# The opening of a hybrid diffusion layer: conditioning pages and context norm written as a pipeline by quarters

## The chip, the cores and the metric

The kernel runs on one core of a Trainium2 chip. The metric is device microseconds of one execution, the median of several runs. A profiled execution, taken apart from those runs, gives the trace from which all durations below come.

The engines are called by the profile's names: PE is TensorE (matmuls; PEld is its weight loads), DVE is VectorE, ACT is ScalarE, POOL is GpSimd, and SP is the engine whose queue issues the DMAs.

## The reference

One layer works on 1024 latent tokens and 256 context tokens with 1024 channels each. A conditioning vector passes through SiLU and one large matrix (`w_ada`, 1024 x 9216, fp32) and gives nine vectors of 1024 values (shift, scale and gate for three sublayers), once for the latent stream and once for the context. The first sublayer is a half SwiGLU feed-forward block, and for the context it reads, cut to what matters:

```python
mods   = split(silu(c)           @ w_ada + b_ada, 9)
mods_c = split(silu(c_ctx)[None] @ w_ada + b_ada, 9)
hn = ctx * rsqrt(mean(ctx * ctx, -1) + 1e-6) * g_ffn1
hn = hn * (1 + mods_c[1]) + mods_c[0]
a, b = split(hn @ w_ffn1_in, 2)          # 1024 -> 2 x 2816
hc = ctx + 0.5 * mods_c[2] * ((silu(a) * b) @ w_ffn1_out)
```

The latent stream goes through the same sublayer, then both through the token mixing (an mLSTM and a spatial-gating branch), and the latent stream through a second feed-forward block and a final norm. All is fp32 at the interface.

## The kernel before

**Number format.** Large products are made in a fast 32-bit matmul format (`fp32r` in the profile) whose operands are split into a high part (ACT casts it) and a low part (DVE subtracts it from the source). The helper `split` (lines 147 to 150) does that. A full product is then three matmuls: high by high, high by low, low by high.

**Where the program starts.** Activations are held with channels on the 128 partitions, so 1024 channels are eight tiles. The program first computes the context's half of the first feed-forward input projection (22 pairs of output tiles `pa` and `pb`, 24 matmuls of 128x256 each: eight channel tiles by three products), and beside it prepares the latent stream. Before any such matmul can run it needs the context's normalized and modulated tiles `hnc`, and these need two things: the reciprocal root of the context's mean square, and the shift and scale vectors out of `w_ada`. This is the opening stage (lines 823 to 956).

**The conditioning pages.** Only the first 2048 of the 9216 columns are needed here. They come in four quarters, each of 256 shift and 256 scale columns. A quarter is eight channel tiles `k` of 128x512. `ada_pages` (L826) fetches them two to a page, each page by two DMAs of 256 KB (in rows of 1 KB). `ada_mm` (L837) splits every `k` into high and low (L841 on ACT, L843 on DVE) and multiplies it with the conditioning vectors as the stationary operand of 4 or 2 columns (L844, L845), accumulating into one PSUM tile `adr`. `ada_out` (L848) copies `adr` to SBUF (L850, ACT), turns its rows into columns with eight small fp32 matmuls (L853, tile `adc`), adds the bias (L857) and forms the scales (L864), for the latent stream (q = 0) and the context (q = 1). `mods0` then calls `mod0` for the quarter's two channel tiles: `Norm.mod` (L231 on) multiplies by scale and norm (L233, DVE), adds the shift on ACT and makes the high and low parts of `hnc`. On even tiles this takes two ACT steps and a POOL subtraction (L235 to L237), on odd ones an ACT and a DVE step (L239, L240).

**The context's norm.** `Norm.sq` squares the eight tiles on ACT (L199, L203) and adds them on DVE (L204). `rstd` sums over partitions with PE (L209), takes the reciprocal root of 128x2 values by Newton steps on DVE (L742 to L751) and spreads the result back over the partitions with a diagonal matrix and PE (L218, L222).

**Weights.** Class `Weights` streams the 44 pages of the projection (512 KB each): `fetch` issues the DMA (L122), `load` splits a page into `hl` (L149, L150), with a ring of four `hl`. The first four pages are fetched between the second and the third quarter. The opening runs `proj_k` (L918 to L922) for the first three output tiles in pieces, as `hnc` tiles become ready. The loop over `f` (L974) then goes on with tile after tile (L176), and queues the latent stream's position add (L901), squares, norm and factor pages behind them.

**What sets the order.** Each engine executes its instructions in the order of its queue. That order is chosen by a scheduler when the program is built: it may move instructions against the order of the code where no data dependence forbids it. Buffers come from pools in rotation: twelve 128x512 tiles `t2` for short-lived values, four PSUM banks `mm`, four `sm`, and eight pages each under `pg0` and `pg1`, which hold conditioning pages first and raw weights afterwards.

**Table warm-ups.** At two places (L700, used twice, and L2033) an activation of one column is written ahead of a norm, to have ACT load the square-root table.

Of the kernel before, what the change touches and what calls it, by code (L numbers as in the profile page):

```python
# [9 lines left out]
F32 = mybir.dt.float32  # L10
# [30 lines left out]

COST = lambda f: getattr(f, 'cost', 512)
# [14 lines left out]
def _build(ctx, tc, nc, a, out):  # L57
# [47 lines left out]

    class Weights:


        def __init__(self, order, name, depth, ahead):
            self.c = ExitStack()  # L110
            self.pool = self.c.enter_context(tc.tile_pool(name=name, bufs=1, reuse_waits="tile"))
            self.order = deque(order)
            self.depth, self.ahead = depth, ahead
            self.raws = deque()
            self.ready = deque()

# [30 lines left out]
    def split(hl, src):  # L147
        dv(hl.shape[-1])
        S.copy(hl[:, 0, :], src)  # L149
        V.tensor_sub(hl[:, 1, :], src, hl[:, 0, :].bitcast(F32))  # L150
# [427 lines left out]
    class Stage:  # L578
# [76 lines left out]
        def outp(self, name, graw, gring, gate, nlo, lo_rows, final, keep, tick=None, halves=1, first=None):  # L655
# [23 lines left out]
            def post(p, pts):  # L679
# [19 lines left out]
                elif p == 6:  # L699
                    S.activation(warm, epst, AF.Sqrt)  # L700
# [57 lines left out]
    c4 = cp.tile([128, 8, 4], F32R, name="c4")  # L758
    ck = sc2.rearrange("p q k -> p k q")
    S.copy(c4[:, :, 0:2], ck)  # L760
    V.tensor_sub(c4[:, :, 2:4], ck, c4[:, :, 0:2].bitcast(F32))
    pick = t2("pick", shape=(4, 2))
# [63 lines left out]
    def ada_pages(qt):  # L826
        pages = []
        for kp in range(NKT // KP):
            pg = hnp.tile([128, KP, 2, QW], F32, name="adapg", tag=f"pg{1 - qt // 2}", bufs=8)
            for i in range(KP):  # L830
                src = a["w_ada"][kp * KP + i].rearrange("p (m c) -> p m c", m=9)[:, 0:2, qt * QW:(qt + 1) * QW]
                nc.sync.dma_start(pg[:, i], src)
            pages.append(pg)
        return pages

    def ada_mm(pages):
        pr = sm_ps("adr")  # L837
        for k in range(NKT):
            src = pages[k // KP][:, k % KP].rearrange("p m c -> p (m c)")
            hi = t2("adhi", F32R)  # L840
            S.copy(hi, src)  # L841
            lo = t2("adlo", F32R)
            V.tensor_sub(lo, src, hi.bitcast(F32))  # L843
            T.matmul(pr[0:4, :], c4[:, k, :], hi, start=k == 0, stop=False, skip_group_check=True)  # L844
            T.matmul(pr[0:2, :], c4[:, k, 0:2], lo, start=False, stop=k == NKT - 1, skip_group_check=True)  # L845
        return pr

    def ada_out(qt, pr):  # L848
        row = t2("adrow", shape=(4, 2 * QW))
        S.copy(row, pr[0:4, :])  # L850
        pc = sm_ps("adc")
        for i in range(2 * QD):
            T.matmul(pc[:, 2 * i:2 * i + 2], row[:, i * 128:(i + 1) * 128], pick, start=True, stop=True)  # L853
        sl = slice(qt * QD, (qt + 1) * QD)
        bv = vs_("b_ada").rearrange("p (m d) -> p m d", m=9)
        for q in range(2):
            V.tensor_add(mods[:, 0:2, q, sl],  # L857
                         pc[:, 0:4 * QD].rearrange("p (m d q) -> p m d q", m=2, q=2)[:, :, :, q], bv[:, 0:2, sl])
            scale_mod(0, 1, q, "g_ffn1", sl)
# [11 lines left out]
    def it(f, *args):  # L871
        return lambda: f(*args)
# [20 lines left out]
    def add_pos(tb, d):  # L893
# [7 lines left out]
        V.tensor_tensor(hv, hv, pv, ALU.add)  # L901

    load_c(hc)
    apg = [ada_pages(0), ada_pages(1)]
    for _ in range(4):
        W.fetch(wfirst)
    apg.append(ada_pages(2))
    apg.append(ada_pages(3))
# [4 lines left out]
    nct = Norm(hc, 256, V)  # L913

    def mod0(d):
        nct.mod(d, smod[:, 0, 1, :], mods[:, 0, 1, :], hnc[d][:, 0, :], hnc[d][:, 1, :])

# [6 lines left out]
    def mods0(qt):  # L924
        ada_out(qt, prs[qt])
        for d in range(qt * QD, (qt + 1) * QD):
            mod0(d)

    for d in range(NKT):
        nct.sq(d)  # L930
    prs = [ada_mm(apg[0])]
    nct.rstd()
    prs.append(ada_mm(apg[1]))
    nct.bcast()
    mods0(0)
    for _ in range(4):
        W.load()
    mods0(1)
    first = [W.take("w1i", i) for i in range(3)]
    pf = [mm_ps("pa")[:, :256] for _ in range(3)]  # L940
    for i in range(3):
        proj_k(pf[i], first[i], range(4))
    prs.append(ada_mm(apg[2]))
    mods0(2)
    prs.append(ada_mm(apg[3]))
    proj_k(pf[0], first[0], (4, 5))
    mods0(3)
    for i in (1, 2):
        proj_k(pf[i], first[i], (4, 5))
# [3 lines left out]

    for i in range(3):
        proj_k(pf[i], first[i], (6, 7))
        W.done(wraw)
# [16 lines left out]

    for f in range(NF):  # L974
# [36 lines left out]
        gated = it(gate_c, f, pa, pb)  # L1011
    gated()
# [1020 lines left out]
    S.activation(warm, epst, AF.Sqrt)  # L2033
# [59 lines left out]
def layout(x, c, ctx, c_ctx, w_ada, b_ada, g_ffn1, w_ffn1_in, w_ffn1_out, g_mix, w_in, b_gates,  # L2093
# [43 lines left out]
    r["wsT"] = np.ascontiguousarray(A(w_s)[0].transpose(2, 0, 1)).reshape(128, 512)  # L2137
    r["w_ada"] = np.ascontiguousarray(A(w_ada)[0]).reshape(8, 128, 9216)
# [32 lines left out]
```

## Time and profile before

| | before |
|---|---|
| median of 3 runs | 2672.95 us (2672.78 to 2678.84) |
| profiled execution | 2675.7 us |
| its span, first to last instruction | 2673.9 us |
| PE busy over the span | 2636.7 us (99%) |
| DVE busy over the span | 2025.6 us (76%) |
| DMA: moved in all | 456.74 MB, mean 171 GB/s |

The share of busy time is a mean over stages. In the first 60 us it is different: by stretches of 10 us, PE is busy 0.01, 7.55, 7.19, 6.16, 7.90 and 9.91 us, though the records of a matmul overlap the next and a busy PE can be a slowly fed one. The column PEclk of the view by windows is the share of the full clock that was granted to PE.

In rows of the timeline the columns are start and length in microseconds, engine, line, operation, output<-input, shapes and count, and in brackets the idle time before and what ended it. Rows of groups read: line, engine, operation, output<-input, shapes, count, then busy time and mean length in ns, then idle time before them.

### The profile page before, as it was taken

What the parts mean: (1) busy time and instruction counts of PE and PEld (TensorE: products, weight loads), DVE (VectorE), ACT (ScalarE), POOL (GpSimd) and SP (SyncE); (2) the same over time, 40 slices, a digit from 0 to 9 for tenths busy, and PEclk for the clock granted to TensorE, in tenths of its full rate; (3) what the DMA queues carried; (4) which work ended last, traced back from release to release, by engine and by line L of the source; (5) the groups of instructions that cost most, each with busy time, mean ns of one, the idle gap of its engine ahead of it and who ended that gap; (6) DMA issues with size and microseconds to landing.
All of it is one profiled execution on the core that took longest, in us unless ns stands there. A gap on an engine that the chain in (4) does not pass through costs nothing.

```text
span 2673.9 us, 35709 instructions
## 1 busy us (share of the span) xinstructions
PE 2636.7 (99%) x12734; PEld 2205.5 (82%) x12734; DVE 2025.6 (76%) x3643; ACT 1103.7 (41%) x1895; POOL 127.6 (5%) x214
## 2 busy tenths in 40 slices
PE   6999999999999999999999999999999999999998
PEld 4998888888889878888888888888887888888887
DVE  6898888788969647788775888677568877776855
ACT  6673333334337525554443342112245433334432
POOL 0000000000000000000000005442000000000000
PEclk9999999999999999999999999999999999999999
DMA  8943454359578222246553477458241433237545
GB/s 276 354 160 107 147 169 138 130 192 319 192 233 278 92 79 90 103 148 215 190 169 110 143 226 268 155 172 284 81 146 35 154 126 130 107 126 271 190 159 172
DMA packets 199585, 456.74 MB, mean 171 GB/s; under 512 B 20592, under 2 KB 49008, under 8 KB 199408
## 3 DMA queue, kind: packets, MB, share of 16 engines
q1 hardware_dynamic: 199408, 454.47, 50.4%
q8 instruction: 100, 1.64, 0.3%
q14 instruction: 77, 0.63, 0.1%
HBM read 328.95 MB, written 125.51 MB: 170 GB/s over the span
## 4 chain that ended last, share of the span: by engine, by line
PE 88%; DVE 5%; DMA 3%; issue 2%; ACT 1%; SPq 0%; POOL 0%; POOLq 0%; ACTq 0%; DVEq 0%
PE qb L401 20%; PE pq L1322 14%; PE po L527 13%; PE qa L401 10%; PE pt L1796 10%; PE pr L1233 6%; PE pa L176 2%; PE pb L176 2%; PE pc L1104 2%; PE pn L1909 2%; PE pu L1635 2%; DMA adapg<-in_w_ada_dram 1%; PE pkc L1302 1%; PE pn L1907 1%; PE pvc L1393 1%
## 5 line engine op out<-in xcount | busy, mean ns | idle before, releaser
L149 ACT CAST ring<-rawq 128x512 fp32r<-128x512 f32 x432 | 265.9, 620 | 533.9 <-PE qb L401 190.3
L527 PE MATMUL po<-gring,wring 128*128 128x512 f32 (+1 forms) x1896 | 425.7, 385 | 1.0 <-DMA gring<-fsp 0.7
L527 PEld LDWEIGHTS po<-gring,wring 128*128 128x128 f32 x1896 | 349.3, 188 | 73.3 <-issue 1.4
L150 DVE TENSOR_TENSOR ring<-rawq,ring 128x512 fp32r<-128x512 f32 x432 | 295.9, 689 | 131.4 <-ACT ring L149 129.6
L401 PE MATMUL qb<-fc,ring 128*128 128x512 f32 x1440 | 339.9, 389 | 0.4 <-DVE u L422 0.2
L401 PEld LDWEIGHTS qb<-fc,ring 128*128 128x128 f32 x1440 | 269.8, 188 | 58.0 <-DVE u L422 2.2
L401 PE MATMUL qa<-fa,ring 128*128 128x512 f32 x1056 | 252.9, 390 | 0.0
L401 PEld LDWEIGHTS qa<-fa,ring 128*128 128x128 f32 x1056 | 198.1, 188 | 41.5 <-issue 0.5
L401 PE MATMUL qb<-fb,ring 128*128 128x512 f32 x984 | 229.8, 389 | 0.0
L401 PEld LDWEIGHTS qb<-fb,ring 128*128 128x128 f32 x984 | 184.6, 188 | 38.4
L1322 PE MATMUL pq<-fc,ring 128*128 128x512 f32 x864 | 212.5, 394 | 0.0
L1322 PEld LDWEIGHTS pq<-fc,ring 128*128 128x128 f32 x864 | 160.9, 188 | 34.6 <-DVE py L1335 0.6
L149 ACT CAST wring<-rw 128x512 fp32r<-128x512 f32 x154 | 95.9, 623 | 224.8 <-PE po L527 192.6
L1796 PE MATMUL pt<-yp,ring 128*128 128x512 f32 x768 | 184.2, 396 | 0.0
L150 DVE TENSOR_TENSOR wring<-rw,wring 128x512 fp32r<-128x512 f32 x154 | 105.6, 686 | 92.9 <-ACT wring L149 92.8
L1796 PEld LDWEIGHTS pt<-yp,ring 128*128 128x128 f32 x768 | 144.1, 188 | 29.3
L1322 PE MATMUL pq<-fa,ring 128*128 128x512 f32 x576 | 142.3, 395 | 0.2 <-ACT px L1328 0.2
L1322 PE MATMUL pq<-fb,ring 128*128 128x512 f32 x576 | 137.7, 393 | 0.0
L1322 PEld LDWEIGHTS pq<-fa,ring 128*128 128x128 f32 x576 | 108.3, 190 | 23.6 <-ACT px L1328 0.6
L1322 PEld LDWEIGHTS pq<-fb,ring 128*128 128x128 f32 x576 | 107.6, 188 | 22.7 <-PE pu L1676 0.3
L149 ACT CAST ring<-rawt 128x512 fp32r<-128x512 f32 x64 | 39.7, 620 | 189.6 <-PE pt L1796 184.0
L780 DVE SCALAR_TENSOR_TENSOR adacc<-adapg,sc,adacc 128x512 f32<-128x512 f32 x140 | 102.7, 746 | 9.2 <-DMA adapg<-in_w_ada_dram 8.6
(351 smaller groups left out, 4128.4 us busy)
## 6 DMA issues: line engine op xcount, KB each, us to landing
adapg<-in_w_ada_dram SPq DMA_DIRECT2D x144, 256.0 KB, 4.3
fsp<-fhl SPq DMA_DIRECT2D x66, 512.0 KB, 2.7
gring<-fsp SPq DMA_DIRECT2D x66, 512.0 KB, 4.0
wraw<-in_w1i_dram SPq DMA_DIRECT2D x44, 512.0 KB, 6.5
graw<-fsp SPq DMA_DIRECT2D x88, 256.0 KB, 3.1
rawq<-in_w1i_dram SPq DMA_DIRECT2D x38, 512.0 KB, 4.2
rawq<-in_w2i_dram SPq DMA_DIRECT2D x38, 512.0 KB, 3.3
fsp<-x SPq DMA_DIRECT2D x66, 256.0 KB, 2.1
```

The source lines that it names most:

```text
L149: S.copy(hl[:, 0, :], src)
L150: V.tensor_sub(hl[:, 1, :], src, hl[:, 0, :].bitcast(F32))
L176: T.matmul(pt, x, y, start=i == 0, stop=i == n - 1)
L401: T.matmul(pt, hl[:, x, sl], pages[p][k][:, y, :], start=first and i == 0, stop=i == 11, skip_group_check=not first)
L527: T.matmul(pt[:, cs], w[:, x, sl], g[:, y, cs], start=grp and kp == 0 and i == 0, stop=kp == NFP - 1 and i == 2, skip_group_check=not grp)
L780: eng.scalar_tensor_tensor(acc, pgt, sc2[:, q, k:k + 1], acc, ALU.mult, ALU.add)
L1104: T.matmul(pt, hl[d // 4][:, x, sl], g[:, y, :], start=f == 0 and d % 2 == 0 and i == 0, stop=f == NF - 1 and i == 2, skip_group_check=True)
L1233: T.matmul(self.pt[m], pg[:, x, sl], hl[:, y, :], start=first and k == 0 and i == 0, stop=k == 3 and i == 2, skip_group_check=not first)
L1322: T.matmul(pt, hl[:, x, k * 128:(k + 1) * 128], pg[k][:, y, :], start=first and k == 0 and i == 0, stop=k == 3 and i == 2, skip_group_chec ...
L1635: T.matmul(pu[:, 0:257], ksl[:, kt * 128:(kt + 1) * 128], wv, start=True, stop=True)
L1796: T.matmul(pt, hl[:, x, k * 128:(k + 1) * 128], pg[:, y, :], start=kh + k + i == 0, stop=kh == 1 and k == 3 and i == 2)
L1909: T.matmul(pn[:, 0:257], qi[:, c_, :], self.C[d][:, c_, :], start=False, stop=c_ == 1)
```

## The change

The opening stage is written anew.

- **Pages.** The host lays the 2048 columns out contiguously (`w_ad0`, 16 pages of 128x1024), and each page comes by one DMA of 512 KB (`ada_page`). The context comes by two DMAs of 512 KB instead of eight of 128 KB. The weights' first four pages are fetched after 14 conditioning pages (one) and after the last (three).
- **Every fourth page in fp32.** For `k` 0 and 4 of a quarter, the 128x512 tile is multiplied as it is, by an fp32 matmul with `cz` (two columns of conditioning and two of zeros), without a split.
- **The norm.** The squares are summed over channels and partitions at once by eight fp32 matmuls with a matrix of ones (`sums_c`); `rstd_c` then computes the reciprocal root on the full 128x256 tile on DVE. The spreading by a diagonal matrix is gone.
- **The order.** `ada_out` ends at the small matmuls; bias and scale are in `ada_mods`, for the context right away and for the latent stream at the end of the stage. Of each quarter, `ada_out` comes after the first page of the next quarter, `mod_a` (bias, scale, first modulation step) after its second page, `mod_b` (the split into `hnc`) after its fourth. `mod_b` has no POOL step and one ACT step per tile instead of two on even tiles.
- **The order is fixed.** Inside `with inorder(last0)` every PE, ACT and DVE instruction is tied behind the one written before it on its engine. For the loop over `f` this holds for PE alone. The latent stream's position adds are tied behind the stage on DVE. Splits of weight pages are tied to one another in order, and the three table warm-ups to the ACT instruction written before them.
- **Ten fp32 matmuls** of a 128x128 matrix of ones by itself (`WARM`) open PE's queue.

```diff
+WARM = 10
+    def follow(i, p):
...
+    @contextmanager
+    def inorder(last, on=None):
+        on = on or (V.engine, S.engine, T.engine)
+        traced = nc.cur_bb.bb.instructions
+        n = len(traced)
+        yield
+        for i in traced[n:]:
+            if i.engine in on:
+                if i.engine in last:
+                    follow(i, last[i.engine])
+                last[i.engine] = i
...
-            split(hl, raw)
+            split(hl, raw, self.last)
...
-                    S.activation(warm, epst, AF.Sqrt)
+                    warm_up(warm)
...
-    def ada_mm(pages):
-        pr = sm_ps("adr")
-        for k in range(NKT):
-            src = pages[k // KP][:, k % KP].rearrange("p m c -> p (m c)")
+    def ada_page(qt, kp):
+        pg = hnp.tile([128, KP, 2, QW], F32, name="adapg", tag=f"pg{1 - qt // 2}", bufs=8)
+        nc.sync.dma_start(pg.rearrange("p k m c -> p (k m c)"), a["w_ad0"][qt * (NKT // KP) + kp])
+        return pg
+
+    def ada_mm(pages, pr, kp):
+        for j in range(KP):
+            k = kp * KP + j
+            src = pages[kp][:, j].rearrange("p m c -> p (m c)")
+            if k % 4 == 0:
+                T.matmul(pr[0:4, :], cz[:, k, :], src, start=k == 0, stop=False, skip_group_check=True)
+                continue
             hi = t2("adhi", F32R)
             S.copy(hi, src)
             lo = t2("adlo", F32R)
             V.tensor_sub(lo, src, hi.bitcast(F32))
...
+    def sums_c():
+        ps_ = sm_ps("sumc")[:, :256]
+        for d in range(NKT):
+            sq = t2("sq")[:, :256]
+            S.activation(sq, hc[d], AF.Square)
+            T.matmul(ps_, ones, sq, start=d == 0, stop=d == NKT - 1)
+        return ps_
+
+    def rstd_c(src):
+        x, z = t2("rsx")[:, :256], t2("rsz")[:, :256]
+        V.tensor_scalar(x, src, 1.0 / D, EPS, ALU.mult, ALU.add)
+        V.tensor_scalar(rsc.bitcast(I32), x.bitcast(I32), -0.5, 1597463007.0, ALU.mult, ALU.add)
+        for _ in range(3):
+            V.scalar_tensor_tensor(z, rsc, -0.5, rsc, ALU.mult, ALU.mult)
+            V.tensor_mul(z, z, x)
+            V.scalar_tensor_tensor(rsc, z, 1.5, rsc, ALU.add, ALU.mult)
...
+    def mod_a(qt):
+        ada_mods(qt, adc[qt], 1)
+        for d in range(qt * QD, (qt + 1) * QD):
+            nts[d] = t2("nt")[:, :256]
+            V.scalar_tensor_tensor(nts[d], hc[d], scc[:, d:d + 1], rsc, ALU.mult, ALU.mult)
+
+    def mod_b(qt):
+        for d in range(qt * QD, (qt + 1) * QD):
+            hi, lo = hnc[d][:, 0, :], hnc[d][:, 1, :]
+            S.activation(hi, nts[d], AF.Identity, bias=shc[:, d:d + 1])
+            V.scalar_tensor_tensor(lo, nts[d], shc[:, d:d + 1], hi.bitcast(F32), ALU.add, ALU.subtract)
...
+    with inorder(last0):
+        wps = sm_ps("wps")
+        for i in range(WARM):
+            T.matmul(wps[:, :128], ones, ones, start=True, stop=True)
+        sc_ = sums_c()
+        pr = sm_ps("adr")
+        ada_mm(apg[0], pr, 0)
+        rstd_c(sc_)
+        for kp in range(1, 4):
+            ada_mm(apg[0], pr, kp)
+        for qt in range(1, NQ):
+            pq, pr = pr, sm_ps("adr")
+            ada_mm(apg[qt], pr, 0)
+            adc.append(ada_out(qt - 1, pq))
+            ada_mm(apg[qt], pr, 1)
+            mod_a(qt - 1)
+            ada_mm(apg[qt], pr, 2)
+            if qt == 3:
+                tile0()
+                proj_k(pf[0], first[0], range(4))
+            ada_mm(apg[qt], pr, 3)
+            mod_b(qt - 1)
+        adc.append(ada_out(3, pr))
+        tile0()
+        proj_k(pf[0], first[0], (4, 5))
+        mod_a(3)
+        mod_b(3)
+        proj_k(pf[1], first[1], range(6))
+        tile0()
+        proj_k(pf[0], first[0], (6, 7))
+        proj_k(pf[1], first[1], (6, 7))
+        for qt in range(NQ):
+            ada_mods(qt, adc[qt], 0)
+        W.load()
+        proj_k(pf[2], first[2], range(NKT))
...
+    pinned = inorder(last0, (T.engine,))
+    pinned.__enter__()
     for f in range(NF):
```

How it moves instructions is seen in the queues. On DVE, between the second quarter and the third, the order before was (`adlo` are the conditioning splits, `hl` the weight splits, `nt` the first modulation step, `mods` and `smod` bias and scale):

```order
L843 TENSOR_TENSOR adlo<-adapg,adhi 128x512 x8
L857 TENSOR_TENSOR mods<-adc,vec 128x2x2 x2
L864 SCALAR_TENSOR_TENSOR smod<-mods,vec 128x2 x2
L233 SCALAR_TENSOR_TENSOR nt<-hc,smod,rb 128x256 x2
L150 TENSOR_TENSOR hl<-wraw,hl 128x1024
L857 TENSOR_TENSOR mods<-adc,vec 128x2x2 x2
L864 SCALAR_TENSOR_TENSOR smod<-mods,vec 128x2
L150 TENSOR_TENSOR hl<-wraw,hl 128x1024 x2
L864 SCALAR_TENSOR_TENSOR smod<-mods,vec 128x2
L233 SCALAR_TENSOR_TENSOR nt<-hc,smod,rb 128x256
L150 TENSOR_TENSOR hl<-wraw,hl 128x1024
L233 SCALAR_TENSOR_TENSOR nt<-hc,smod,rb 128x256
```

In the changed kernel DVE has, from the end of the norm to the second modulated quarter (`rsc` is the norm, L987 the last step to `hnc`):

```order
L972 SCALAR_TENSOR_TENSOR rsc<-rsz,rsc 128x256
L873 TENSOR_TENSOR adlo<-adapg,adhi 128x512 x8
L888 TENSOR_TENSOR mods<-adc,vec 128x2x2
L895 SCALAR_TENSOR_TENSOR smod<-mods,vec 128x2
L981 SCALAR_TENSOR_TENSOR nt<-hc,smod,rsc 128x256 x2
L873 TENSOR_TENSOR adlo<-adapg,adhi 128x512 x3
L987 SCALAR_TENSOR_TENSOR hnc<-nt,mods,hnc 128x256 x2
L873 TENSOR_TENSOR adlo<-adapg,adhi 128x512 x3
L888 TENSOR_TENSOR mods<-adc,vec 128x2x2
```

The four weight splits between two quarters are gone from there, each quarter has six conditioning splits instead of eight, and a quarter's chain stands among the next quarter's splits.

On PE, the end of the stage before (`pa` and `pb` are the context's projection):

```order
L845 MATMUL adr<-adlo,c_100 2x512
L922 MATMUL pa<-hnc,hl 128x256 x6
L853 MATMUL adc<-pick,adrow 128x2 x4
L922 MATMUL pa<-hnc,hl 128x256 x12
L176 MATMUL pb<-hnc,hl 128x256 x9
L922 MATMUL pa<-hnc,hl 128x256 x18
L176 MATMUL pb<-hnc,hl 128x256 x15
```

and in the changed kernel:

```order
L868 MATMUL adr<-adapg,cz 4x512
L874 MATMUL adr<-adhi,c_100 4x512
L875 MATMUL adr<-adlo,c_100 2x512
L952 MATMUL pa<-hnc,hl 128x256 x12
L874 MATMUL adr<-adhi,c_100 4x512
L875 MATMUL adr<-adlo,c_100 2x512
L874 MATMUL adr<-adhi,c_100 4x512
L875 MATMUL adr<-adlo,c_100 2x512
L882 MATMUL adc<-pick,adrow 128x2 x4
L952 MATMUL pa<-hnc,hl 128x256 x60
L205 MATMUL pb<-hnc,hl 128x256 x24
```

Of the first three tiles' 72 projection matmuls, 36 stood before the last two quarters' results and 36 around the last small matmuls; now 12 stand inside the fourth quarter and 60 in one piece behind the last small matmuls.

More of the change, by code (lines that the diff above doesn't have):

```diff
@@ L1 @@
 from collections import deque
-from contextlib import ExitStack
+from contextlib import ExitStack, contextmanager
 import numpy as np
@@ L104, in sm_ps, with warm_up @@
         return ps.tile([128, 512], F32, name=name, tag="sm", bufs=4)
+    def follow(i, p):
+        if not isinstance(i, mybir.Instruction):
+            i = i.ins
+        tc.add_manual_dep(i, p.name, mybir.DependencyInfo(mybir.DependencyClass.NoSync, mybir.DependencyReason.DATA),
+                          reason="inorder")
+    @contextmanager
[9 more added lines that the diff above has]
+                last[i.engine] = i
+    def warm_up(t):
+        e = S.engine
+        p = [i for i in nc.cur_bb.bb.instructions if i.engine == e][-1]
+        follow(S.activation(t, epst, AF.Sqrt), p)
     class Weights:
@@ L115, in __init__ @@
             self.ready = deque()
+            self.last = [None, None]
         def fetch(self, page):
@@ L145, in dv, with split @@
         debt[0] += 62 + 0.77 * w
-    def split(hl, src):
+    def split(hl, src, last=None):
         dv(hl.shape[-1])
-        S.copy(hl[:, 0, :], src)
-        V.tensor_sub(hl[:, 1, :], src, hl[:, 0, :].bitcast(F32))
+        ins = S.copy(hl[:, 0, :], src).ins, V.tensor_sub(hl[:, 1, :], src, hl[:, 0, :].bitcast(F32)).ins
+        if last is not None:
+            for i, p in zip(ins, last):
+                if p is not None:
+                    follow(i, p)
+            last[:] = ins
     todo = deque()
@@ L758, in _build @@
     c4 = cp.tile([128, 8, 4], F32R, name="c4")
+    cz = cp.tile([128, 8, 4], F32, name="cz")
+    G.memset(cz, 0.0)
     ck = sc2.rearrange("p q k -> p k q")
@@ L843, in ada_mm @@
             V.tensor_sub(lo, src, hi.bitcast(F32))
-            T.matmul(pr[0:4, :], c4[:, k, :], hi, start=k == 0, stop=False, skip_group_check=True)
+            T.matmul(pr[0:4, :], c4[:, k, :], hi, start=False, stop=False, skip_group_check=True)
             T.matmul(pr[0:2, :], c4[:, k, 0:2], lo, start=False, stop=k == NKT - 1, skip_group_check=True)
-        return pr
     def ada_out(qt, pr):
@@ L941, in _build @@
[L941 to L949, printed above, removed]
+    rsc = cp.tile([128, 256], F32, name="rsc")
+    def sums_c():
[5 more added lines that the diff above has]
+        return ps_
@@ new lines, in rstd_c @@
+    def rstd_c(src):
+        x, z = t2("rsx")[:, :256], t2("rsz")[:, :256]
+        V.tensor_scalar(x, src, 1.0 / D, EPS, ALU.mult, ALU.add)
+        V.tensor_scalar(rsc.bitcast(I32), x.bitcast(I32), -0.5, 1597463007.0, ALU.mult, ALU.add)
+        for _ in range(3):
+            V.scalar_tensor_tensor(z, rsc, -0.5, rsc, ALU.mult, ALU.mult)
+            V.tensor_mul(z, z, x)
+            V.scalar_tensor_tensor(rsc, z, 1.5, rsc, ALU.add, ALU.mult)
+    scc, shc = smod[:, 0, 1, :], mods[:, 0, 1, :]
@@ new lines, in _build, with tile0 @@
+    first, pf, adc = [], [], []
+    def tile0():
+        W.load()
+        first.append(W.take("w1i", len(first)))
+        pf.append(mm_ps("pa")[:, :256])
+    last0 = {}
+    with inorder(last0):
[29 more added lines that the diff above has]
+        proj_k(pf[1], first[1], (6, 7))
+        for qt in range(NQ):
+            ada_mods(qt, adc[qt], 0)
+        W.load()
+        proj_k(pf[2], first[2], range(NKT))
@@ L2032, in _build @@
         n_.act = True
-    S.activation(warm, epst, AF.Sqrt)
+    warm_up(warm)
     def fin_o(dt, tb, pt):
```

55 lines of the change are left out of this document (18 added, 37 removed).

## The prediction

> **What bounds the kernel now.** I read the page first, then the chain of waits over the first 182 us, then stretches of 2 us.
>
> ```profile
> span 2673.9 us, 35709 instructions
> PE 2636.7 (99%) x12734; PEld 2205.5 (82%) x12734; DVE 2025.6 (76%) x3643; ACT 1103.7 (41%) x1895; POOL 127.6 (5%) x214
> ```
>
> PE is the bound over the span, so time can only come out of stretches in which PE is not fed. The chain (start, length, what) shows where the first one ends:
>
> ```profile
> 7.93 6.43 DMA adapg<-in_w_ada_dram
> ...
> 59.91 1.05 ACT hl L149
> ...
> 61.28 3.14 PE pa L176 x24
> 64.42 2.88 PE pb L176 x24
> ...
> 116.62 0.79 PE p L209 x8
> ...
> 128.47 0.86 PE rb L222 x2
> ...
> 180.22 1.84 PE qa L401 x8
> ```
>
> Until 61.28 the chain goes through pages, splits and single steps. From there to 180.22, where the latent projection begins, it is PE without a gap, one tile of 24 matmuls every 2.88 us (0.12 each). At 61.28 four of the 44 tiles are done, which are worth 11.52 us of full-speed PE. So the projection stands as if it had begun at 61.28 - 11.52 = 49.76 and never paused. That is the number to compare: whatever the change does to this equivalent start goes one for one to the end, as long as PE stays fed behind it.
>
> **The change part by part.** The durations are in these groups of the first 62 us, and in single rows of the timeline:
>
> ```profile
> L843 DVE TENSOR_TENSOR adlo<-adapg,adhi 128x512 fp32r<-128x512 f32 x32 | 20.7, 686 | 3.6 <-ACT adhi L841 3.3
> L233 DVE SCALAR_TENSOR_TENSOR nt<-hc,smod,rb 128x256 f32<-128x256 f32 x8 | 3.6, 477 | 0.1
> L204 DVE TENSOR_TENSOR acc<-acc,sq 128x256 f32<-128x256 f32 x7 | 3.0, 425 | 1.8 <-ACT sq L203 1.2
> L850 ACT COPY adrow<-adr 4x512 f32<-4x512 f32 x4 | 2.3, 575 | 5.5 <-PE adr L845 5.5
> ```
>
> ```profile
> 1.62 3.75 SPq L891 DMA_DIRECT2D hc<-in_cT_dram  x8
> 8.23 0.75 ACT L203 ACTIVATE sq<-hc 128x256 f32<-128x256 f32 x2 [1.14 <-DMA hc<-in_cT_dram]
> 18.42 0.16 DVE L749 SCALAR_TENSOR_TENSOR rs_z<-rs_y 128x2 f32<-128x2 f32 x1
> 18.62 0.16 DVE L750 TENSOR_TENSOR rs_z<-rs_z,rs_x 128x2 f32<-128x2 f32 x1
> 26.45 0.87 DVE L233 SCALAR_TENSOR_TENSOR nt<-hc,smod,rb 128x256 f32<-128x256 f32 x2
> 34.16 0.63 PE L844 MATMUL adr<-adhi,c 128*4 128x512 f32 x1
> 34.58 0.63 PE L845 MATMUL adr<-adlo,c 128*2 128x512 f32 x1
> 39.27 1.05 PE L853 MATMUL adc<-pick,adrow 4*128 4x2 f32 x8 [0.66 <-ACT adrow L850]
> 44.39 2.68 ACT L841 CAST adhi<-adapg 128x512 fp32r<-128x512 f32 x5
> 45.62 3.09 DVE L843 TENSOR_TENSOR adlo<-adapg,adhi 128x512 fp32r<-128x512 f32 x5
> 49.30 0.39 PE L844 MATMUL adr<-adhi,c 128*4 128x512 f32 x1
> 49.53 0.40 PE L845 MATMUL adr<-adlo,c 128*2 128x512 f32 x1
> 59.09 3.50 DVE L150 TENSOR_TENSOR hl<-wraw,hl 128x1024 fp32r<-128x1024 f32 x3 [2.63 <-ACT hl L149]
> ```
>
> Five splits in 3.09 us are 0.61 each on DVE; casts go at 0.52 on ACT. A 512-wide matmul follows the last after 0.23 us (49.30 to 49.53), or after 0.42 when PE is slow (34.16 to 34.58). An fp32 matmul 512 wide took 0.86 us on PE (the `rb` piece of the chain), and I take 1.7 when slow.
>
> Why PE is slow at times is in the next view (after the stretch: busy time of PE, PEld, DVE, ACT and POOL, then PEclk, DMA share, GB/s):
>
> ```profile
> 4.00:6.00 2.00, 0.00 (x0) 0.00 (x0) 0.60 (x2) 1.38 (x7) 0.00 (x0) 1.00 0.78 245
> 22.00:24.00 2.00, 2.00 (x8) 0.29 (x8) 2.00 (x4) 1.86 (x3) 0.00 (x0) 1.00 1.01 401
> 28.00:30.00 2.00, 0.00 (x0) 0.00 (x0) 2.00 (x6) 2.00 (x3) 0.00 (x0) 0.91 1.09 347
> 34.00:36.00 2.00, 2.00 (x6) 0.58 (x5) 2.00 (x4) 1.44 (x3) 0.00 (x0) 0.50 1.10 350
> 36.00:38.00 2.00, 2.00 (x10) 0.63 (x7) 1.97 (x4) 1.24 (x2) 0.00 (x0) 0.89 1.09 363
> 44.00:46.00 2.00, 2.00 (x10) 2.00 (x11) 2.00 (x3) 2.00 (x6) 1.42 (x2) 0.50 1.03 412
> 50.00:60.00 10.00, 9.91 (x72) 8.30 (x71) 3.39 (x9) 3.90 (x8) 0.74 (x1) 1.00 0.03 10
> 60.00:120.00 60.00, 59.68 (x499) 59.48 (x498) 53.16 (x87) 36.91 (x60) 0.00 (x0) 1.00 0.99 364
> 120.00:180.00 60.00, 60.00 (x492) 59.04 (x491) 58.26 (x103) 42.99 (x71) 0.00 (x0) 1.00 0.61 200
> ```
>
> PE stands idle through 28 to 30, the granted clock drops to 0.50, and it is back at 36 to 38, some 3.6 us after matmuls restart.
>
> *Sums.* The eight context DMAs take 3.75 us to issue, and the last squares waited for data until 8.23. The same 1 MB in two DMAs, at the 245 GB/s of the row 4 to 6, lands about 7.2 (6.5 to 8.3). Four squares at 0.37 (two in 0.75) and a last fp32 matmul of 0.43 plus its drain end at 9.3 if the ten warm-up matmuls have brought the clock up; if not, eight at 0.86 from about 5.7 end at 12.6. I take 9.9, near the first end, since the warm-ups keep PE busy from about 1 us on, longer than those 3.6 us.
>
> *Norm.* `rstd_c` is eleven DVE steps that depend on one another, where the old ones had two columns (0.16 long, 0.20 apart, so 0.04 between). Six of 0.48 and five of 0.42 (rows L233, L204), each with 0.04, are 5.4 us, on the path: the splits behind it in DVE's fixed order wait. It ends at 15.3 (14 to 18).
>
> *Rest of the first quarter.* PE has nothing to do from about 11 to 16, so by the row 28 to 30 it loses its clock. First split done at 16.0; then a low matmul, a pair, an fp32 one and a pair, five at 0.43 and one at 1.7, to 19.9; with the clock back, four at 0.23 to 20.8. The copy `adrow` (0.58) ends at 21.4, PE does the next quarter's first fp32 matmul and pair until 22.1, the small matmuls take 1.05, and DVE starts `mods` at 23.3. With the clock kept it would be 21.0.
>
> *A quarter in steady order.* On DVE: six splits 3.66, `mods` and `smod` 0.4, two `nt` 0.87, two `hnc` steps 0.87 as for `nt`, and about 0.2 of waiting: 6.0 us. Beside it PE needs 12 x 0.23 + 2 x 0.86 + 1.05 = 5.5, ACT 6 x 0.52 + 0.58 + 2 x 0.4 = 4.5, and the pages 2.1 MB at 401 GB/s 5.2. DVE is the bound, PE close behind; all pages are there by about 30, ahead of their splits. Two more quarters bring `mods` of the third to 35.3.
>
> *End of the stage.* `nt` and `mods` 1.3, a split 0.6, a weight split 1.2 (a third of 3.50), two splits 1.2: 39.6. PE has done the twelve projection matmuls (1.44) by then, finishes two pairs at 40.7, `adrow` 41.3, small matmuls 42.35. From there PE has 24 projection matmuls, 2.9 us, to 45.25; the fourth quarter's chain (`mods`, `nt`, ACT step 0.5, `hnc` step) is done at 45.1, just covered. Equivalent start: 42.35 - 1.44 = 40.9. Against 49.76 that is **8.9 us earlier**, and 2672.95 - 8.9 = 2664.0. The profiled execution with its 2675.7 lies 2.7 above that median, its span 0.95; the difference is made inside the span and carried over to the median.
>
> *Edits at nothing.* The latent stream's scales move to the end (eight steps of 0.2 on DVE), under PE's 24 matmuls of the third tile. The tied splits of weight pages keep the order that they have. The table warm-ups change which ACT step precedes a table load of 1.28 us in the norms later on; PE is inside 2.88 us tiles or longer runs there, and I price it at 0, with 1 us either way. SP's queue now issues all sixteen latent pages right behind the eight weight pages, where before it stood still from 43 to 60 (row 50 to 60: 10 GB/s); that takes load off the stretch 60 to 120, where DMA was at 0.99, and can only help.
>
> **The rivals.**
>
> *1. PE at half clock through the whole stage: slower.* In the quarters PE works in bursts between DVE's splits. Then a quarter is 12 x 0.43 + 2 x 1.7 + 1.5 (small matmuls, an estimate above their 1.05) = 10.0 us on PE in place of DVE's 6.0. Sums at 12.6, norm 18.0, first quarter's PE to 25, three quarters and twelve slow matmuls to 57.6, copy and small matmuls to 59.7: equivalent start 58.3, and 1.7 more until the clock is back, 60.0. That is 10.2 us later, 2683. It decides from the point at which the bursts no longer count as busy. For it: at 44 to 46 the clock was 0.50 while PE worked without a gap, after 4 us in which it did little. Against it: at 22 to 24 eight matmuls of 0.23, under half of the time, kept 1.00, and the new quarters fill 5.5 of 6.0 us. The Trainium skill (TensorE: Matmul & The Clock Gate, A second HAM failure mode: psum-queue depth-cycling) says that frequent short idle times between groups of matmuls let the gate swing between half and full rate. By that rule this rival would be the forecast, or half of it, at about 2673; the trace speaks against it with the row 22 to 24. Chance 0.06.
>
> *2. Given back on DVE: 2668.* DVE is busy 111.4 of the 120 us from 60 to 180, PE 119.7. The norm's sums (`p`, 116.62) now stand behind 531 context matmuls where they stood behind 555, and PE's order is fixed, so PE would wait there for DVE's squares. DVE's queue has 21 weight splits (1.17), 30 steps of 512 (0.61) and 20 of 256 (0.38) up to them, 50 us, and starts at 48, PE arrives at 40.9 + 531 x 0.12 = 104.6. Before, the same list took DVE from 59 (its row above) to 116, 57 us; at that pace it is 0.5 us late. A wait of 4 us leaves 2668. Chance 0.15.
>
> *3. The pages come late: 2670.* Context, sixteen pages and one weight page are 10.1 MB. At the 245 GB/s of the row 4 to 6, from 2.5 us on, the last page lands at 44; casts, two pairs, copy and small matmuls behind it take 4.3 us, less the 1.44: start 46.6, a gain of 3.2. At 300 GB/s it lands at 36, ahead of DVE's 39.6, and costs nothing. The 245 was reached with DMAs of 128 KB issued 0.47 us apart, the 401 at 22 to 24 with weight pages of 512 KB among them, so only the worst case hurts. Chance 0.06.
>
> *4. Clock and sums at their good ends.* Sums at 9.3, no lost clock in the first quarter: 0.6 + 2.3 earlier, 2661. Part of the forecast's own spread.
>
> **How the numbers follow.** The forecast with its spread (sums 12.6 in place of 9.9 gives 2666.7, unseen buffer waits of 1 to 2 us in the fixed order 2668; the good ends 2661, a shorter norm and table loads 2659.5) has 0.73, and its middle is **2664.0**. Range 2659.5 to 2669.5, which takes in rival 2 and leaves out 1 and 3. A measurement of this kernel can tell about 0.3%, 8.0 us, from no change, so the line is 2664.9, close to the forecast. Of the forecast's 0.73, 0.53 lies below it, the rest above; rivals 2 and 3 are within the 8 us; rival 1 and accidents 0.06 are slower. Faster 0.53, same 0.41, slower 0.06.
>
> **What would show it.** First `mods` of the context at 21 to 24 us; the next two about 6.0 apart, with DVE near full and PEclk at 1.00; a dip of PEclk at 12 to 20; the first run of 60 `pa` matmuls from about 42 with no wait before the fourth quarter's; the latent projection `qa` at 171 in place of 180.2. Wrong would be: quarters of 8 us or more with PE as what DVE waits for (rival 1); PE waiting at the norm's sums near 105 (rival 2); casts that wait for pages after 25 us (rival 3); or `qa` at 171 and the end unmoved, which would put the loss behind the context's projection.

## The result and the profile after

| | before | after |
|---|---|---|
| median of runs taken together | 2674.03 us (4 runs, 2672.78 to 2678.84) | 2690.6 us (4 runs, 2689.69 to 2691.19) |
| ratio | | 1.0058, interval 1.0041 to 1.0076 |
| span of the profiled execution | 2673.9 us | 2689.4 us |
| first latent projection matmul `qa` | 180.22 us | 170.43 us |

The forecast was 2664.0 us, with a range of 2659.5 to 2669.5. The kernel became 0.6% slower instead, although the stage that was rewritten became faster by more than the forecast. The page of the changed kernel opens with its span and engines:

```profile
span 2689.4 us, 35675 instructions
PE 2663.2 (99%) x12764; PEld 2211.0 (82%) x12764; DVE 2023.5 (75%) x3631; ACT 1096.0 (41%) x1882; POOL 125.3 (5%) x211
```

PE is as full as before, at 99%, but it is busy for 26.5 us more, while the span grew by 15.5. Idle time of PE is therefore not what was added. The chain of waits of the changed kernel (start, length, what), from the norm to the latent projection:

```profile
6.57 3.73 PE sumc L962 x16
10.33 0.44 DVE rsx L967
...
41.17 1.05 PE adc L882 x8
42.22 1.14 PE pa L952 x8
43.37 1.68 PE pa L952 x12
45.05 0.95 ACT hl L174
46.02 1.24 DVE hl L174
47.30 2.88 PE pa L952 x22
50.18 2.84 PE pb L205 x24
53.03 2.85 PE pa L205 x24
...
104.65 0.79 PE p L238 x8
...
170.43 16.32 PE qa L430 x72
```

The chain leaves its last single step, a split of weights (`hl`), at 47.30, where before it left it at 61.28. No wait stands before the norm's sums `p` at 104.65, and `qa` starts 9.79 us earlier than at 180.22. One detail is new: a tile of the context's projection takes 2.85 us, not 2.88. The timeline of the changed kernel has the start of `mods` for the context, quarter by quarter:

```profile
22.95 0.16 DVE L888 TENSOR_TENSOR mods<-adc,vec 128x4 f32<-128x4 f32 x1
29.00 0.16 DVE L888 TENSOR_TENSOR mods<-adc,vec 128x4 f32<-128x4 f32 x1
35.06 0.16 DVE L888 TENSOR_TENSOR mods<-adc,vec 128x4 f32<-128x4 f32 x1
```

The quarters are 6.05 us apart. The view by stretches (stretch, busy time of PE, PEld, DVE, ACT and POOL, then PEclk, DMA share, GB/s) has PE's clock beside it:

```profile
10.00:16.00 6.00, 2.15 (x8) 0.35 (x7) 5.55 (x14) 3.51 (x6) 0.00 (x0) 0.93 1.02 409
16.00:20.00 4.00, 4.00 (x10) 0.60 (x9) 2.84 (x5) 0.00 (x0) 0.00 (x0) 0.67 1.03 410
...
24.00:30.00 6.00, 6.00 (x25) 1.99 (x24) 5.64 (x13) 4.54 (x10) 0.00 (x0) 1.00 1.03 412
30.00:36.00 6.00, 6.00 (x25) 1.93 (x25) 5.64 (x13) 4.76 (x9) 0.00 (x0) 1.00 1.03 399
```

The clock is lost once, behind the norm, and stays at 1.00 through the quarters, with DVE busy 94% of the time.

So 25.3 us were lost behind 170.43 (the 15.5 of the span and the 9.79 gained before), where the program's matmuls are the same, in the same order but for a single one that moved by seven places. The last piece of PE in the chain shows the loss most plainly, as nothing waits in it; first the kernel before:

```profile
2444.98 176.81 PE po L527 x780
```

and the kernel after:

```profile
2455.31 181.28 PE po L556 x780
```

The same 780 matmuls take 226.7 ns each before and 232.4 ns after (start to start, below called the pitch), at a granted clock of 1.00 in both (the stretch 2440 to 2615). The groups of the profile say the same of the large projections. Before (busy time, mean ns of one):

```profile
L527 PE MATMUL po<-gring,wring 128*128 128x512 f32 x1800 | 412.1, 390 | 0.8 <-DMA gring<-fsp 0.5 <-ACT px L684 0.3
L401 PE MATMUL qb<-fc,ring 128*128 128x512 f32 x1440 | 339.9, 389 | 0.4 <-DVE u L422 0.2
L1796 PE MATMUL pt<-yp,ring 128*128 128x512 f32 x768 | 184.2, 396 | 0.0
L1233 PE MATMUL pr<-ring,fc 128*128 128x512 f32 x288 | 66.1, 390 | 0.0
```

After:

```profile
L556 PE MATMUL po<-gring,wring 128*128 128x512 f32 x1800 | 416.6, 393 | 0.6 <-DMA gring<-fsp 0.4 <-ACT fa L174 0.2
L430 PE MATMUL qb<-fc,ring 128*128 128x512 f32 x1440 | 344.1, 392 | 0.4 <-DVE u L451 0.4
L1879 PE MATMUL pt<-yp,ring 128*128 128x512 f32 x768 | 184.3, 396 | 0.0
L1316 PE MATMUL pr<-ring,fc 128*128 128x512 f32 x288 | 67.6, 395 | 0.0
```

`po`, `qb` and `pr` grew; `pt<-yp,ring`, the same shape with the same ring, did not. That speaks against a slower clock or memory in general, and for something that differs by pairs of operands.

What differs is the address. The change adds two tiles to the pool of constants, `cz` (128 B per partition) and `rsc` (1024 B). The pools that are laid out behind the constants from the low end of SBUF (`hn`, `t2`, `w1`, `x`) moved up by 1152 B; those laid out from the high end stayed. 1152 is 4 x 256 + 128. I joined the start-to-start times of consecutive matmuls on PE with the addresses of their tiles in the built program (the profile has no addresses), and sorted them by the moving operand's address less the stationary one's, modulo 256. For `qb<-fc,ring`, where `fc` stayed and some of the buffers of `ring` moved, matmuls that kept a difference of 0 took 227.3 ns after, and those that went to 128 took 233.0. `pt<-yp,ring` reads both operands from pools that moved together, and kept its pitch, so a move by itself is not what counts. That the pitch follows the difference is the theory that the experiments test.

### The profile page after: what moved, and what is told of

It reads as the page before. It is cut to its first block, busy times and chain, and to the rows that moved or that the text cites. A ratio compares the mean times of both kernels' runs of the same rounds, so it can differ in the third digit from the quotient of the medians.

```text
span 2689.4 us, 35675 instructions
## 1 busy us (share of the span) xinstructions
PE 2663.2 (99%) x12764; PEld 2211.0 (82%) x12764; DVE 2023.5 (75%) x3631; ACT 1096.0 (41%) x1882; POOL 125.3 (5%) x211
## 4 chain that ended last, share of the span: by engine, by line
PE 90%; DVE 4%; DMA 3%; issue 2%; ACT 1%; POOL 0%; SPq 0%; POOLq 0%; DVEq 0%; ACTq 0%
PE qb L430 20%; PE pq L1405 15%; PE po L556 14%; PE qa L430 10%; PE pt L1879 9%; PE pr L1316 6%; PE pb L205 2%; PE pc L1187 2%; PE pa L205 2%; PE pn L1992 2%; PE pu L1718 2%; PE pkc L1385 1%; PE pvc L1476 1%; PE pn L1990 1%; PE pm L1836 1%
```

## The experiments

Three theories stood at the start. A: the pitch of a matmul depends on the difference of its operands' addresses modulo 256 ("phase" in the expectations). B: any move of the pools costs. C, the rival without addresses: the order that the change fixes on the engines leaves a worse pattern of traffic behind the opening. And the prediction's own steps on the opening had to be tried.

**An unused 128 B in the changed kernel: the shift is then 1280, five times 256.**

```diff
     epst = cp.tile([128, 1], F32, name="epst")
+    cp.tile([128, 32], F32, name="pad")
```

> The changed kernel with an unused tile of 128 bytes per partition more among the constants, so that the pools behind them start 1280 bytes later than before the change instead of 1152; the order of instructions is the same. Theory A (phase): a matmul of 512 columns is 5.7 ns slower when the addresses of its two SBUF operands differ by 128 modulo 256 bytes, and the change put the pools hn, t2, w1 and x 1152 = 4 x 256 + 128 bytes further while fx, h and rg stayed. Then 1280 = 5 x 256 restores the phase: pitch of 36 qb matmuls 8.16 us, context tiles back at 2.88 us, qa at about 171.7, time about 2665.5 us, ratio to before 0.997. Theory B (any move of the pools costs, by what the addresses then share): 2690, as changed. Theory C (the earlier start or the fixed order brings PE, DVE and DMA into a worse relation in time): 2690, pitch 8.27 to 8.5.

Measured: 2669.64 us against 2676.03 for before, ratio 0.9977 (0.9967 to 0.9986). More unused memory makes the kernel about 21 us faster than the changed kernel. B and C, which expected 2690, fall here. The time is 4 us above that of theory A; the opening of this execution was late, which comes back at the run without warm-ups.

**An unused 1152 B in the kernel before, with nothing else of the change.**

```diff
     epst = cp.tile([128, 1], F32, name="epst")
+    cp.tile([128, 288], F32, name="pad")
```

> The kernel before with an unused tile of 1152 bytes per partition among its constants, nothing else changed, and the order of instructions the same. Theory A: the loss behind the context's projection (25.3 us between qa and the end) appears without the change's code, less about 1.3 us that the context's 256-wide matmuls gain: about 2698 us, ratio 1.009. Theory B: the same. Theory C: 2674, ratio 1.000.

Measured: 2693.97 us, ratio 1.0065 (1.0053 to 1.0078). The chain of this kernel ends with PE's

```profile
2458.79 181.28 PE po L528 x780
```

the same 181.28 as in the changed kernel. The pad alone, without any change of order, costs 17.9 us. It is not all of what was lost behind `qa`: in this trace `qa` starts at 181.16 and the span is 2692.1 us, so 17.3 us more than before lie behind `qa`, where the changed kernel has 25.3 more. Theory A had put all of the 25.3 down to addresses, and its 2698 (ratio 1.009) was too high.

**The same with 1280 B.**

```diff
     epst = cp.tile([128, 1], F32, name="epst")
+    cp.tile([128, 320], F32, name="pad")
```

> The kernel before with an unused tile of 1280 bytes per partition. Theory A: 1280 is a multiple of 256, the phases are those of before: 2674 us, ratio 1.000. Theory B: like 1152 bytes, about 2698. Theory C: 2674.

Measured: 2675.08 us, ratio 1.0 (0.999 to 1.0009). A larger move than the last costs nothing. So the remainder counts, not the move.

**The changed kernel with `cz` and `rsc` in a pool of their own,** opened above `w1` for the opening alone, so that all other pools lie as before.

```diff
-    cz = cp.tile([128, 8, 4], F32, name="cz")
...
+    nc_ = ExitStack()
+    np_ = nc_.enter_context(tc.tile_pool(name="nrm", bufs=1, reuse_waits="tile"))
+    cz = np_.tile([128, 8, 4], F32, name="cz")
...
-    rsc = cp.tile([128, 256], F32, name="rsc")
+    rsc = np_.tile([128, 256], F32, name="rsc")
...
+    nc_.close()
     n1 = [Norm(h[tb], 512, V) for tb in range(2)]
```

> The changed kernel with its two new constant tiles in a pool of their own above the weights' pool, closed at the end of the opening stage, so that every other pool lies where it lay before the change; order of instructions the same as changed. Theories A and B: about 2665.5 us, ratio 0.997. Theory C: 2690, ratio 1.006.

Measured: 2667.65 us, ratio 0.9975 (0.9965 to 0.9985). The chain of this kernel:

```profile
52.70 2.88 PE pa L205 x24
...
171.38 16.35 PE qa L430 x72
...
2436.75 176.81 PE po L556 x780
```

The context tiles are back at 2.88, `po` is back at 176.81, and `qa` is 8.84 us earlier than at 180.22: the forecast's 8.9. The same kernel in a later set of runs, on another chip:

> The kernel with the two new constant tiles in a pool of their own once more, to stand on the same chip as the next run. Theory A: as before, ratio 0.997 to 0.998, about 2667.

Measured: 2673.0 us against 2674.68, ratio 0.9992 (0.9983 to 1.0), which does not repeat the 0.9975. The single runs overlap (2665.86 to 2675.08 the first time, 2668.97 to 2676.04 the second). The profiled executions of the two differ by 8.1 us of span (2666.2 and 2674.3) for one and the same program, and the view of PE's waits from 800 to 1600 shows part of it. The first time (who waited for what: us in all, times, longest):

```profile
PE pvc L1479 <- DVE nt L262: 0.8, 1, 0.8
PE pc L1190 <- DMA gc<-gcsp: 0.7, 1, 0.7
PE pm L1839 <- DMA vnp<-vnsp: 0.6, 1, 0.6
PE p L238 <- DVE acc L233: 0.2, 1, 0.2
```

The second time:

```profile
PE pm L1839 <- DMA vnp<-vnsp: 2.1, 1, 2.1
PE pc L1190 <- ACT wring L174: 1.3, 1, 1.3
PE pq L1408 <- DVE py L1421: 1.3, 1, 1.3
PE pu L1762 <- ACT wv L1745: 1.1, 1, 1.1
PE pvc L1479 <- DVE nt L262: 0.8, 1, 0.8
PE pvc L1479 <- DVE ring L174: 0.5, 1, 0.5
```

That is 7.1 us of waits in place of 2.3. The rest is PE's clock, in two stretches of the second execution that stood at 1.00 in the first:

```profile
988.00:996.00 8.00, 8.00 (x43) 6.74 (x43) 2.38 (x8) 4.67 (x8) 0.00 (x0) 0.79 0.00 0
1592.00:1600.00 8.00, 8.00 (x41) 7.31 (x41) 7.27 (x12) 3.95 (x7) 3.58 (x9) 0.79 0.61 225
```

Each dip is worth 8 x 0.21 = 1.7 us. Of such dips the changed kernel's profiled execution has two, that of the kernel before one, and the first of this kernel none. One and the same program shows them in one execution and not in another; whether the chip has a part in it was not tried.

**The opening's own steps.** In the kernel with the pool of its own, the two fp32 pages of each quarter are split like the other six:

```diff
-            if k % 4 == 0:
-                T.matmul(pr[0:4, :], cz[:, k, :], src, start=k == 0, stop=False, skip_group_check=True)
-                continue
...
-            T.matmul(pr[0:4, :], c4[:, k, :], hi, start=False, stop=False, skip_group_check=True)
+            T.matmul(pr[0:4, :], c4[:, k, :], hi, start=k == 0, stop=False, skip_group_check=True)
```

> The changed kernel with its two new constant tiles in a pool of their own, and with the two fp32 pages of each quarter split into high and low like the other six (arithmetic as in the kernel before). Theory of the prediction (DVE paces a quarter: six splits in 6.0 us, so eight splits need 7.2): the first `mods` of the context comes about 1.2 us later, the next two 7.2 to 7.3 us apart instead of 6.05, `qa` starts 4.5 to 5 us later than in the run with the pool of its own, and the time is that run's 2667.7 plus 4.7, about 2672.4, ratio to before 0.9992. Rival (PE paces it: two fp32 matmuls of 0.86 us are replaced by four of 0.23, so a quarter gets shorter): `mods` under 6.0 us apart and 2666 to 2667.

Measured: 2670.38 us against 2674.21, ratio 0.9987 (0.9979 to 0.9996). Its timeline:

```profile
22.68 0.15 DVE L882 TENSOR_TENSOR mods<-adc,vec 128x4 f32<-128x4 f32 x1
29.82 0.16 DVE L882 TENSOR_TENSOR mods<-adc,vec 128x4 f32<-128x4 f32 x1 [0.27 <-PE adc L876]
36.95 0.16 DVE L882 TENSOR_TENSOR mods<-adc,vec 128x4 f32<-128x4 f32 x1 [0.23 <-PE adc L876]
```

Quarters of 7.14 us where eight splits were forecast at 7.2: DVE paces them. The first `mods` comes no later than with fp32 pages (22.56 in the first run with the pool of its own); one fp32 matmul that is gone had taken 1.69 us at half clock in the changed kernel, which would explain it. So `qa` is at 174.24, 2.9 us later instead of 4.7: the theory's pace is right, its first quarter was not. In this trace the granted clock also fell to 0.50 inside the quarters, once, from 30.0 to 33.4 us; the quarter that it fell into still took 7.13 us.

Without the warm-up matmuls:

```diff
-        wps = sm_ps("wps")
-        for i in range(WARM):
-            T.matmul(wps[:, :128], ones, ones, start=True, stop=True)
```

> The changed kernel with its two new constant tiles in a pool of their own, and without the ten fp32 matmuls that open PE's queue. Theory of the prediction (PE is slow until it has been busy for some 3.6 us, so the norm's eight sums take 0.86 us each and end at 12.6 instead of 10.3): `rsx` starts at 12.3 to 12.8, everything behind it in the opening is 2 to 2.5 us later, `qa` at 172.5 to 173, time 2667.7 plus 2.3, about 2670. Rival (the sums wait for the context's data and the squares, not for PE's clock): `rsx` within 0.5 us of 10.33 and no difference, 2667.7.

Measured: 2670.55 us, ratio 0.9986 (0.9978 to 0.9995). In the timeline the eight sums take 5.99 us where they took 3.72 with the warm-ups (x16 in these rows, since an fp32 matmul is recorded as two):

```profile
6.16 5.99 PE L964 MATMUL sumc<-sq,ones 128*128 128x256 f32 x16 [6.16 <-ACT sq L963]
...
12.18 0.42 DVE L969 TENSOR_SCALAR rsx<-sumc 128x256 f32<-128x256 f32 x1 [2.37 <-PE sumc L964]
```

`rsx` comes 2.27 us later than in the first run with the pool of its own (9.91), and `qa` at 173.84, 2.46 us later. The sums start 0.85 us apart up to about 10.6 us and 0.44 apart behind it, as at half and at full clock; the column PEclk shows 1.00 throughout, so the clock is inferred from these lengths.

The warm-ups do not work every time. The run with 128 B more has all ten, and its chain reads

```profile
6.53 5.72 PE sumc L963 x16
```

with `rsx` at 12.27 and `qa` at 173.84, as late as here. So the clock's step of the forecast has the right size, but its condition, that the warm-ups bring the clock up in time, failed in one of the seven profiled executions that have them. Why is open. The total times of these two kernels cannot be told from the second run with the pool of its own; their traces can.

**The other differences.** An unused 64 B, then 192 B, in the kernel before.

```diff
     epst = cp.tile([128, 1], F32, name="epst")
+    cp.tile([128, 16], F32, name="pad")
```

> The kernel before with an unused tile of 64 B per partition in the constants' pool: the pools behind it move by 64 B. Theory A with the pitches read from the two first profiles (512-column matmuls, moving operand's address less the stationary one's, modulo 256: 0 gives 227.0 ns, 64 gives 229.3, 192 gives 233.5): 2244 matmuls at 192 are 14.6 us, 1092 at 64 are 2.5 us, and 132 of `pq` leave 192, -0.9: 16 us slower, about 2690, ratio 1.006. Theory A2 (only multiples of 128 matter, 64 is near enough to none): 2674, ratio 1.000. Theory A3 (any difference costs the same 5.7 ns, whatever its size and sign): 3336 x 5.7 ns = 19 us, 2693.

Measured: 2688.08 us against 2674.21, ratio 1.0052 (1.004 to 1.0065). From its chain, one tile of the context's projection and the last run of `po`:

```profile
70.29 2.72 PE pb L177 x24
...
2452.12 182.01 PE po L528 x780
```

```diff
     epst = cp.tile([128, 1], F32, name="epst")
+    cp.tile([128, 48], F32, name="pad")
```

> The kernel before with an unused tile of 192 B per partition in the constants' pool, the mirror of the run with 64 B: the 2244 matmuls of 512 columns that were 192 apart there are 64 apart here, and the 1092 that were 64 apart are 192 apart. Theory A with a sign (64 gives 229.2 ns, 192 gives 233.4, 0 gives 227.0): 2244 x 2.2 + 1092 x 6.4 = 4.9 + 7.0 = 11.9 us on those; the matmuls of 256 columns at 64 are between no change and the 3.9 us gain that they had at 192, so 8 to 12 us slower, 2682 to 2686, `po` of the last stage (780 matmuls, 176.81 us in the kernel before) at 178.5, where at 192 it was 181.8 or so. Theory A3 (size of the difference without sign, as in a ring of 256): as the run with 64 B, 2688.

Measured: 2688.56 us against 2674.68, ratio 1.0054 (1.0041 to 1.0066), and

```profile
2456.57 178.55 PE po L528 x780
```

`po` does what A with a sign says to 0.05 us: 178.55 where 64 B the other way gave 182.01. So A2 and A3 fall. The total alone would have fitted A3 (2688). It was 2.6 us above the range that A with a sign gave: 64 apart cost 229.7 ns on the mean of its 2140 gaps and not 229.2, and matmuls that stayed at 0 took 228.1 ns and not 227.0.

All the pitches together, worked out from the gaps of consecutive matmuls and the addresses as above (mean ns, and how many gaps):

```
moving less stationary,
modulo 256               0             64            128           192
512 columns, before      227.0 (8576)                              233.5 (351)
512 columns, after       227.5 (5391)  229.1 (121)   232.8 (3181)  233.6 (231)
512, before + 64 B       227.5 (5514)  230.0 (1040)                233.3 (2370)
512, before + 192 B      228.1 (5391)  229.7 (2140)  231.8 (128)   233.4 (1271)
256 columns, before      119.8 (1749)
256 columns, after       119.8 (233)                 118.7 (1523)
256, before + 64 B       119.9 (229)                               116.2 (1509)
256, before + 192 B      119.8 (227)   117.0 (1501)
```

With 512 columns, 0 is best and 192 worst. With 256 columns, 0 is worst. Summed over the program's matmuls (1104 and 2244 of 512 columns that moved, 5688 that stayed at 0, 132 that had been at 192, and 1632 of 256 columns), the table gives about 14 us for the pad of 64 B and for that of 192 B; 13.9 was measured for both.

The table also shows that the difference is not all for 512 columns either: matmuls that stayed at 0 took 0.5 to 1.1 ns more in its three kernels with moved pools. What does this was not tried.

**A version that uses both.** The kernel before has 396 `pq` matmuls 192 apart (their buffer `ring2` lies in a pool whose other tiles leave it so), and 256-column matmuls at 0. First a pad of 128 B ahead of the context's `hl`, and 64 B in the pool of `ring2`:

```diff
             self.pool = self.c.enter_context(tc.tile_pool(name=name, bufs=1, reuse_waits="tile"))
+            self.pool.tile([128, 32], F32, name="pad")
...
     st.part(ns, 3, beside)
+    fl("pad2", "pad2", (128, 16), F32, 1)
```

> The changed kernel with its two new constant tiles in a pool of their own, and two unused pads: 128 B ahead of the `hl` ring of the context's projection (1056 matmuls of 256 columns then have operands 128 apart modulo 256; in the changed kernel such a matmul took 118.6 ns, in the kernel before 120.3) and 64 B in the pool of `ring2`, which puts the 396 matmuls `pq` that read it from 192 apart to in phase (233.5 ns to 227.0). Theory A (the address difference modulo 256 sets the pitch): 1056 x 1.7 ns + 396 x 6.5 ns = 1.8 + 2.6 = 4.4 us less than the run with the pool of its own, 2663.3, ratio to before 0.9958; `pq` with `ring2` at 227 ns, `pa` and `pb` 2.85 us a tile. Rival (these pitches belong to their places in the program, such as DMA traffic beside them, not to the addresses): 2667.7, ratio 0.9975.

Measured: 2666.86 us against 2674.21, ratio 0.9971 (0.9961 to 0.9981). No 512-column matmul gap of this kernel is at 192 any more, and 8936 are at 0, with 227.0 ns. Against the run with the pool of its own the span fell by 1.6 us, not by 4.4: the context's part came (`qa` at 170.77 in place of 171.38, although the single steps ended 0.7 us later), but PE's idle time behind 300 us, summed over the trace, was 13.2 us in place of 10.7, which takes back what `pq` gained. That may be chance: the second execution of the kernel with the pool of its own had over 14 us of it. Then with 64 B ahead of `hl`:

```diff
-            self.pool.tile([128, 32], F32, name="pad")
+            self.pool.tile([128, 16], F32, name="pad")
```

> As the run with two pads, but the pad ahead of the context projection's `hl` is 64 B instead of 128, so that the moving operand `hnc` lies 192 above the stationary one modulo 256, where the kernel before with its pools moved by 64 B took 116.3 ns a matmul of 256 columns in place of 120.0. Theory A: the 1056 matmuls of the context gain 3.9 us and the 396 `pq` with `ring2` 2.6, `pa` and `pb` stand 2.79 us apart, `qa` starts 3.9 us earlier than in the kernel with the pool of its own (but for what the opening differs); the whole is 6.5 us less if nothing is given back at waits later on, 3.9 if what `pq` gains is given back as in the run with 128 B; so 2660.5 to 2663. Rival (the 116.3 ns came with that run's other conditions): tiles of 2.85 us as with 128 B, 2666.

Measured: 2664.29 us against 2674.68, ratio 0.9961 (0.9948 to 0.9975), the fastest version of the study, and 1.3 us above the range expected. Its context tiles:

```profile
52.69 2.83 PE pa L206 x24
55.52 2.83 PE pb L206 x24
...
169.26 16.35 PE qa L431 x72
```

`qa` is 2.1 us earlier than at 171.38, not 3.9. 2.83 us is less than 2.85 with 128 B, but more than the 2.72 with the same difference in the kernel before plus 64 B (117.6 against 116.2 ns). So the difference modulo 256 is not all that sets the pitch of 256-column matmuls; what else does was not tried.

## Why the prediction was wrong

**The opening: right.** The norm's sums were forecast at 9.9 and ended at 10.30; the norm took 4.9 us, not 5.4, which cancels it; the first `mods` was forecast at 23.3 and came at 22.95, the next ones 6.05 apart against 6.0; the small matmuls ended at 42.22 against 42.35. The equivalent start, 50.18 - 3 x 24 x 0.12, is 41.5 against 40.9. PE worked on while the two splits of `hl` ran that stand in the chain at 45.05 and 46.02; the difference is made of short pauses among the 60 projection matmuls, five of 0.1 to 0.3 us, the longest just before 47.30, where PE waits for the second of these splits. The forecast had no pause there. `qa` was forecast at 171 and came at 170.43, of which about 1 us is the 256-column matmuls' gain by address.

**Rivals 1 to 3: not seen.** The quarters kept the full clock. The Trainium skill (TensorE: Matmul & The Clock Gate, A second HAM failure mode: psum-queue depth-cycling) tells of a kernel whose gate swung at frequent short idle times; here the rows 24 to 36 show 1.00. Only the kernel with eight splits a quarter had one fall of the clock in them, and its quarters were no longer for it. `p` did not wait at 104.65, and DMA ran at 399 to 412 GB/s.

**The step that failed** is the first part's last sentence: "whatever the change does to this equivalent start goes one for one to the end, as long as PE stays fed behind it". PE stayed fed, and its matmuls became slower. The step took the pitch of an instruction that the change doesn't touch as fixed. The term that is missing from the sum belongs under "Edits at nothing", and the two new tiles of the constants' pool do not appear there, although the diff shows where `cz` is read. As they live as long as the kernel, they moved every pool behind them.

What it is worth, from the changed program's counts and the table: 3348 matmuls of 512 columns went from 0 to 128, x 5.8 ns = 19.4 us; 132 went from 192 to 64, -0.6; the 5688 that stayed at 0 took 0.5 ns more, 2.8; 576 of 256 columns behind `qa` gained 1.1 each, -0.6. That is 21.0 of the 25.3 us lost behind `qa`. One more dip of the clock is 1.7, and the view of waits adds about 2 (`pm` waited 2.5 us for `vnp`, before 1.2; `pc` 1.0 for `gc`, before not).

The prediction named how it would look, "`qa` at 171 and the end unmoved, which would put the loss behind the context's projection", but gave it no chance of its own and no mechanism.

**What the change is worth without the addresses.** The placements that keep the remainder give 0.9977, 0.9975 and 0.9992, that is 2 to 8 us where 8.9 was forecast. In the first two, on one chip, the gain of the opening seems to go to the end, as the step that failed would have it (one trace each): with 128 B more, `qa` is 6.4 us earlier (173.84) and the median 6.4 us lower; with the pool of its own, 8.8 and 8.4. In the second run of the pool of its own, on another chip, `qa` is 8.4 us earlier (171.87), but the median only 1.7 us lower. What that profiled execution gives back stands in PE's waits between 800 and 1600 and in two dips of the clock, which differ by several microseconds between executions. Whether the earlier start makes them longer on the average stays open; no run isolates it.

## What to carry to other kernels

Before pricing a change to a full kernel, compare the addresses of the large operands before and after, not only the instructions: a small tile added to a long-lived pool can move every pool behind it. Where the moving and the stationary operand come from pools that move apart, count the matmuls and multiply by the change of pitch; here 5.8 ns on 3348 matmuls outweighed a stage that was rewritten. A tile that is needed only for a stage belongs in a pool that closes with the stage, and a difference of speed between two versions is compared with an unused pad in either before it is put down to their order.

## What the runs showed of the hardware that was not expected

- A 512-column matmul of split operands took 227.0 ns with its two SBUF operands' addresses equal modulo 256 (227.5 to 228.1 in three kernels with moved pools), 229 to 230 at 64, 232 to 233 at 128 and 233.5 at 192 (moving less stationary), at a granted clock of 1.00. The sign counts: in the run of 780 `po`, 178.55 us at 64, 182.01 at 192, 176.81 at 0. What in the chip makes the difference count, no run here shows.
- A 256-column matmul is slowest in phase: 119.8 ns at 0, 118.7 at 128, 117.0 at 64 and 116.2 or 117.6 at 192.
- One program's executions, on two chips, differed by 8.1 us of span, of which 3.4 were two dips of PE's clock at 988 and 1592 us.
- Ten fp32 matmuls of 128 columns ahead of the norm's sums brought these from 5.99 us to 3.72, but in one of seven profiled executions they still took 5.72.
